# A fourth chunk pair with seven products, weight low parts made by accumulating transfers, and the first tile's parts ahead at stage borders

## Chip, core and metric

The kernel runs on one core of a Trainium2 chip. The metric is device time in microseconds (us) of one execution. The engines of the core are TensorE (PE in the profile), VectorE (DVE), ScalarE (ACT), GpSimd (POOL) and SyncE (SP); SyncE and GpSimd issue the DMA transfers here.

## The reference, cut to what matters

Two layers of an encoder over 256 tokens with 2048 features, all in float32:

```python
def hybrid_layer(x, ...):
    h = rmsnorm(x, pre_mix_norm)
    proj = h @ w_in                                     # 2048 -> 4176
    ...                                                 # attention, convolution, gated DeltaNet
    mix = jnp.concatenate([o_a, o_b, o_c], axis=-1) @ w_out
    x = x + rmsnorm(mix, post_mix_norm)
    h = rmsnorm(x, pre_ffn_norm)
    f = (jax.nn.silu(h @ w_gate) * (h @ w_up)) @ w_down # 2048 -> 5632 -> 2048
    return x + rmsnorm(f, post_ffn_norm)
```

`rmsnorm(x, w)` is `x * rsqrt(mean(x^2) + eps) * w`, with a mean per token and a gain `w` per feature.

## The kernel before, in words

**Products.** Every float32 operand is split into a high part (a rounded copy) and a low part (the rest): `hilo` (L327) lets ScalarE copy the high part (L328, CAST) and VectorE subtract it from the source (L329). A product of a 128x128 piece of activations with a 128x512 piece of weights is then three matmuls: high by high, low by high, high by low. The 256 tokens are two tiles of 128 (t = 0 and 1).

**Weights.** They stream from HBM once, as 512 KB transfers of two 128-row chunks into `ws` tiles (128x1024), issued by SyncE (L410). From a `ws` the two halves `wh` and `wl` are made. There are five slots each of `ws`, `wh` and `wl` (`WSB`, `WHB`, L42 and L43); whoever wants a new tile waits until a slot's last reader is done, and slots go round in the order in which they come free.

**Stages of a layer.** Input projection (`dense`, L337), the mixers, the output projection (`out_proj`, L1180, with `residual`, L477, at its end), the feed-forward's gate and up products, and `w_down` through `out_proj` again. At each border between stages the rows `xs` are transposed in groups of four chunks (`norm_quad`, L431): TensorE transposes (L435), and eight small instructions of 128x128 on ScalarE (L332) and VectorE (L333) apply the gain and split. The per-token factor of the norm is applied at the products' end. `norm_tok` makes all four groups of a tile at once.

**Gate and up.** The 5632 columns are 11 blocks of 512. The first block of a layer goes through `dense`; the other ten through `gate_up` (L1277; 20 calls in the two layers). Such a block takes the 16 chunks in eight pairs, in the order `QORDER` (L45). A pair multiplies two tiles of tokens by two chunks of the gate weight and two of the up weight: eight products, 24 matmuls. For the pairs in `FAST` (L44) it is done with seven products, 21 matmuls, as in Strassen's scheme: VectorE combines the weights (L1341 to L1347), and the sums of activations are made once per layer by `token_sums` (L1230), spread over other work. An eight-product pair takes two `wh`/`wl` slots, a seven-product pair four (in the order `r1`, `r2`, `r32`, `r14`). All 24 or 21 matmuls stand in one line, L1302. After the last pair the block's results are combined, SiLU and product applied, and the result is transposed later as a background task (`turn`, L1220), whose place the number `EARLY` (L46) decides for the first blocks.

**What sets the order.** The code is written as one instruction list; a scheduler orders each engine's instructions, and each engine then executes its own list in order, waiting on semaphores for the others.

Of the kernel before, what the change touches and what calls it, by code (L numbers as in the profile page):

```python
# [16 lines left out]
P = 128  # L17
# [3 lines left out]
NT = 2  # L21
# [22 lines left out]
FAST = (0, 1, 2)  # L44
QORDER = (4, 0, 5, 1, 6, 2, 7, 3)  # L45
EARLY = 2  # L46
# [7 lines left out]
def kernel(  # L54
# [282 lines left out]
    def dense(lhs, ks, n, load, evac, ch=2, need=None, pre=None, head=0, mid=None, tail=0,  # L337
              gain=None):
# [17 lines left out]
        def unit(u):  # L356
# [7 lines left out]
            with ExitStack() as order:  # L364
                if u < head:
                    for u0, ins in hold:
                        if u >= u0:
                            order.enter_context(tc.issue_after(ins.ins))
                if gain is None:
                    hilo(wh[:, 0:m * n], wl[:, 0:m * n], ws[:, 0:m * n])  # L370
                else:
                    for c in range(m):
                        sl = slice(c * n, (c + 1) * n)
                        hilo_col(wh[:, sl], wl[:, sl], ws[:, sl], vcol(*gain, kc[c]))
# [56 lines left out]
    def norm_quad(t, g, tiles, gain=None):  # L431
# [5 lines left out]
        if gain is None:  # L437
            hilo(hi, lo, ps)
        else:
# [53 lines left out]

    for l in range(DEPTH):
        hT = {}

        def more(g, t):

            for n in range(1, min(g + 2, 4)):
                if (n, 0) not in hT:  # L500
                    load_x(0, n)
                    norm_quad(0, n, hT, (0, PRE_MIX))
        hl = quad_lhs(hT, None if l else more)

        def mid_mix():
# [3 lines left out]
            norm_tok(1, hT, (l, PRE_MIX))  # L509
# [3 lines left out]
        if l:  # L513
            norm_tok(0, hT, (l, PRE_MIX))
        else:
# [664 lines left out]
        def out_proj(lhs, passes, w, wpm, rname, need=None):  # L1180
            parts = {}
            ssqp = [SM(4, "ssqp0"), SM(4, "ssqp1")]
            for i, ks in enumerate(passes):
                last = i == len(passes) - 1
                for nb in range(4):
# [3 lines left out]
                    def ev(t, ps):  # L1189
# [16 lines left out]
        out_proj(lmix, passes, w_out[l], wpm, "rm", need_mix)  # L1206


        h2 = {}
        h2l = quad_lhs(h2)  # L1210
        norm_tok(0, h2, (l, PRE_FFN))
# [18 lines left out]
        def token_sums():  # L1230
# [46 lines left out]
        def gate_up(fb, par):  # L1277
# [38 lines left out]

            def half(w, q):
# [14 lines left out]
            for n, q in enumerate(QORDER):  # L1332
# [58 lines left out]
        def first_block():  # L1391
# [6 lines left out]
            def ev_u(t, ps):  # L1398
# [4 lines left out]
                  mid=lambda: norm_tok(1, h2, (l, PRE_FFN)))  # L1403
# [13 lines left out]
        out_proj(quad_lhs(hid), [list(range(44))], w_down[l], wpf, "rd", lambda k: [f"hid{k // 4}"])  # L1417
    for t in range(NT):
# [34 lines left out]
```

## Time and profile before

| what | value |
|---|---|
| median of 3 runs | 2237.43 us (2236.23 to 2238.26) |
| the profiled execution's own time | 2236.18 us |
| its span, first to last instruction | 2234.4 us |
| outside the span | 1.8 us |
| mean granted TensorE clock | 0.998 of full speed |
| TensorE busy | 2201.4 us (99%), 10483 matmuls |
| VectorE / ScalarE / GpSimd busy | 79% / 54% / 2% |
| DMA | 407.76 MB, 182 GB/s over the span |

The first rows of a profile to read are the busy shares and the chain of work that ended last: they tell which engine sets the time. After that one stage at a time is read, with windows (busy time of each engine in a stretch), groups of instructions, and timelines.

### The profile page before, as it was taken

What the parts mean: (1) busy time and instruction counts of PE and PEld (TensorE: products, weight loads), DVE (VectorE), ACT (ScalarE), POOL (GpSimd) and SP (SyncE); (2) the same over time, 40 slices, a digit from 0 to 9 for tenths busy, and PEclk for the clock granted to TensorE, in tenths of its full rate; (3) what the DMA queues carried; (4) which work ended last, traced back from release to release, by engine and by line L of the source; (5) the groups of instructions that cost most, each with busy time, mean ns of one, the idle gap of its engine ahead of it and who ended that gap; (6) DMA issues with size and microseconds to landing.
All of it is one profiled execution on the core that took longest, in us unless ns stands there. A gap on an engine that the chain in (4) does not pass through costs nothing.

```text
span 2234.4 us, 29364 instructions
## 1 busy us (share of the span) xinstructions
PE 2201.4 (99%) x10483; PEld 1837.9 (82%) x10483; DVE 1765.2 (79%) x2943; ACT 1196.4 (54%) x1726; POOL 45.7 (2%) x93
## 2 busy tenths in 40 slices
PE   8999999999999999999999999999999999999998
PEld 7888887788888888888879888877788888888886
DVE  6777998899989897544486779978999998975444
ACT  6665545655555555444366655456555555554442
POOL 2000000000000000000000000000000000000000
PEclk9999999999999999999999999999999999999999
DMA  7554525546656656555556545245556566565553
GB/s 251 169 181 144 186 98 163 160 161 208 216 180 217 226 191 221 171 195 192 178 173 185 182 142 175 95 151 161 188 197 217 191 216 213 202 215 178 191 196 123
DMA packets 218546, 407.76 MB, mean 182 GB/s; under 512 B 17607, under 2 KB 30065, under 8 KB 218400
## 3 DMA queue, kind: packets, MB, share of 16 engines
q1 hardware_dynamic: 215360, 397.72, 54.3%
q0 software_dynamic: 3008, 8.16, 1.3%
q8 instruction: 82, 1.34, 0.2%
q14 instruction: 64, 0.52, 0.1%
q10 hardware_dynamic: 32, 0.01, 0.0%
HBM read 402.94 MB, written 2.90 MB: 182 GB/s over the span
## 4 chain that ended last, share of the span: by engine, by line
PE 91%; DVE 5%; DMA 1%; ACT 1%; issue 1%; SPq 0%; DVEq 0%; ACTq 0%; POOLq 0%
PE acc L1302 18%; PE tp L1302 18%; PE acc L352 16%; PE acc L354 16%; PE acc L353 16%; DVE wl L329 1%; DVE xs L482 1%; PE tp L1224 1%; DVE u L944 1%; DMA cd<-u 1%; PE tp L1045 0%; PE tp L796 0%; PE tp L789 0%; PE tp L1016 0%; ACT wh L328 0%
## 5 line engine op out<-in xcount | busy, mean ns | idle before, releaser
L328 ACT CAST wh<-ws 128x1024 fp32r<-128x1024 f32 (+3 forms) x820 | 813.8, 1010 | 803.5 <-PE acc L353 410.5
L329 DVE TENSOR_TENSOR wl<-ws,wh 128x1024 fp32r<-128x1024 f32 (+3 forms) x820 | 942.4, 1170 | 347.7 <-ACT wh L328 340.8
L352 PE MATMUL acc<-wh,u 128*128 128x512 f32 (+2 forms) x1792 | 696.8, 390 | 1.8 <-ACT u L332 1.8
L354 PE MATMUL acc<-wl,u 128*128 128x512 f32 (+2 forms) x1792 | 686.9, 383 | 2.5 <-DVE wl L329 2.5
L353 PE MATMUL acc<-wh,u 128*128 128x512 f32 (+2 forms) x1792 | 686.4, 383 | 3.0 <-DVE sm L264 2.7
L354 PEld LDWEIGHTS acc<-wl,u 128*128 128x128 f32 x1792 | 337.4, 188 | 67.2 <-DVE wl L329 4.7
L353 PEld LDWEIGHTS acc<-wh,u 128*128 128x128 f32 x1792 | 337.8, 189 | 65.8 <-DVE sm L264 3.6
L352 PEld LDWEIGHTS acc<-wh,u 128*128 128x128 f32 x1792 | 337.9, 189 | 63.3 <-ACT u L332 3.6
L1302 PE MATMUL tp<-wh,u 128*128 128x512 f32 x1220 | 375.9, 390 | 1.1 <-DVE u L329 0.9
L1302 PE MATMUL acc<-wh,u 128*128 128x512 f32 x1220 | 375.5, 389 | 0.0
L1302 PEld LDWEIGHTS tp<-wh,u 128*128 128x128 f32 x1220 | 228.4, 188 | 50.3 <-DVE u L329 1.7
L1302 PEld LDWEIGHTS acc<-wh,u 128*128 128x128 f32 x1220 | 228.7, 188 | 47.7 <-ACT wh L328 0.3
L1302 PE MATMUL acc<-wl,u 128*128 128x512 f32 x610 | 237.1, 389 | 0.0
L1302 PE MATMUL tp<-wl,u 128*128 128x512 f32 x610 | 236.4, 389 | 0.0
L1302 PEld LDWEIGHTS acc<-wl,u 128*128 128x128 f32 x610 | 114.5, 188 | 24.1 <-DVE wl L329 0.2
L1302 PEld LDWEIGHTS tp<-wl,u 128*128 128x128 f32 x610 | 114.4, 188 | 24.1
L944 DVE SCALAR_TENSOR_TENSOR u<-u,cols 128x241 f32<-128x241 f32 (+14 forms) x240 | 101.0, 469 | 0.0
L1340 ACT CAST wh<-ws 128x1024 fp32r<-128x1024 f32 x60 | 63.0, 1050 | 26.2 <-PE tp L1302 11.2
L332 ACT ACTIVATE u<-tp,cols 128x128 fp32r<-128x128 f32 (+2 forms) x116 | 40.1, 392 | 32.0 <-DVE u L333 28.3
L1341 DVE TENSOR_TENSOR wl<-ws,wh 128x512 fp32r<-128x512 f32 x60 | 41.1, 686 | 19.2 <-ACT wh L1340 18.9
L1325 ACT ACTIVATE u<-u,sm 128x512 f32<-128x512 f32 x40 | 28.8, 724 | 32.5 <-DVE u L1372 22.1
L333 DVE SCALAR_TENSOR_TENSOR u<-tp,cols,u 128x128 fp32r<-128x128 f32 (+2 forms) x116 | 39.6, 377 | 4.9 <-ACT u L332 4.9
(301 smaller groups left out, 1548.2 us busy)
## 6 DMA issues: line engine op xcount, KB each, us to landing
ws<-in_w_gate_dram SPq DMA_DIRECT2D x176, 512.0 KB, 4.9
ws<-in_w_up_dram SPq DMA_DIRECT2D x176, 512.0 KB, 4.8
ws<-in_w_down_dram SPq DMA_DIRECT2D x176, 512.0 KB, 3.6
ws<-in_w_in_dram SPq DMA_DIRECT2D x112, 512.0 KB, 4.4
ws<-in_w_out_dram SPq DMA_DIRECT2D x64, 512.0 KB, 3.7
ws<-in_w_ukv_dram SPq DMA_DIRECT2D x16, 512.0 KB, 3.7
ws<-in_w_uq_dram SPq DMA_DIRECT2D x16, 384.0 KB, 3.4
ws<-in_w_in_dram SPq DMA_DIRECT2D x10, 444.0 KB, 4.0
```

The source lines that it names most:

```text
L328: act.copy(out=hi, in_=src)
L329: dve.tensor_tensor(out=lo, in0=src, in1=hi.bitcast(F32), op=ALU.subtract)
L332: ins = act.activation(out=hi, in_=src, func=AF.Identity, scale=col)
L333: dve.scalar_tensor_tensor(out=lo, in0=src, scalar=col, in1=hi.bitcast(F32), op0=ALU.mult, op1=ALU.subtract)
L352: pe.matmul(o, xh, rh, start=(i == 0), stop=False)
L353: pe.matmul(o, xl, rh, start=False, stop=False)
L354: pe.matmul(o, xh, rl, start=False, stop=(i == len(ks) - 1))
L944: dve.scalar_tensor_tensor(out=o, in0=i, scalar=wc, in1=o, op0=ALU.mult, op1=ALU.add)
L1302: pe.matmul(o, a, b, start=count[i] == 1, stop=count[i] == total[i])
L1325: act.activation(out=sg[t], in_=x, func=AF.Silu, scale=rfb[0][:, t:t + 1])
L1340: act.copy(out=wh, in_=wg)
L1341: dve.tensor_tensor(out=wl[:, 0:512], in0=b11, in1=wh[:, 0:512].bitcast(F32), op=ALU.subtract)
```

## The change

- `FAST` gets pair 3 as a fourth seven-product pair. The order of pairs becomes 4, 0, 5, 1, 2, 6, 3, 7: pairs 1 and 2, both with seven products, now stand next to each other. `EARLY` becomes 1.
- In the four eight-product pairs the up weight's low part is not subtracted by VectorE any more. In `split_dma` ScalarE copies the high part as before (L1324), writes its negative into `wl` (L1325), and GpSimd issues a transfer of the same 512 KB of `w_up` from HBM that is added onto `wl` in place (L1326). That is 40 such transfers per layer. The up weight's `ws` is still loaded, for the high part.
- `norm_quad`: except for the first group of tile 0, VectorE multiplies the whole transposed 128x512 by the gain (L448) and `hilo` splits the result, one instruction each instead of four. The product is kept for `token_sums`, which then needs no addition of high and low part. Groups are made when a product asks for them (`ask`).
- At three borders the first group of the next stage's tile 0 (`after0`) stands ahead of tile 1's work in the last `dense`; at the kernel's end tile 0's stores do.

The diff, cut to its core:

```diff
-FAST = (0, 1, 2)
-QORDER = (4, 0, 5, 1, 6, 2, 7, 3)
-EARLY = 2
+FAST = (0, 1, 2, 3)
+QORDER = (4, 0, 5, 1, 2, 6, 3, 7)
+EARLY = 1
...
         if pre is not None:
             pre()
+        if after0 is not None:
+            after0()
         for t in range(1 if tail else 0, NT):
             evac(t, acc[t][:, 0:n])
...
-    def norm_quad(t, g, tiles, gain=None):
+    def gain_cols(l, i, c, n):
+        if l == 0 and i == PRE_MIX:
+            return col0[:, c:c + n]
+        o = voff[(l, i)] + c
+        return cols[:, 0, o:o + n]
+
+    def norm_quad(t, g, tiles, gain, keep=None):
 
         ps = TP()
         for c in range(4):
             pe.transpose(ps[:, c * P:(c + 1) * P], xs[:, t, (4 * g + c) * P:(4 * g + c + 1) * P], ident)
         hi, lo = U(F32R), U(F32R)
-        if gain is None:
-            hilo(hi, lo, ps)
-        else:
+        if g == 0 and t == 0:
             for c in range(4):
                 s = slice(c * P, (c + 1) * P)
-                ins = hilo_col(hi[:, s], lo[:, s], ps[:, s], vcol(*gain, 4 * g + c))
-                if not tiles:
-                    first_hi.append(ins)
+                ins = hilo_col(hi[:, s], lo[:, s], ps[:, s], vcol(*gain, c))
+                first_hi.append(ins)
+        else:
+            f = U()
+            dve.tensor_tensor(out=v3(f, 4), in0=v3(ps, 4), in1=bc(gain_cols(*gain, 4 * g, 4), 2, P), op=ALU.mult)
+            hilo(hi, lo, f)
+            if keep is not None:
+                keep[(g, t)] = f
         tiles[(g, t)] = (hi, lo)
 
-    def norm_tok(t, tiles, gain=None):
-        for g in range(4):
-            norm_quad(t, g, tiles, gain)
+    def ask(tiles, gain, load=None, keep=None):
+
+        def more(g, t):
+            for n in range(min(g + 2, 4)):
+                if (n, t) not in tiles:
+                    if load is not None and t == 0:
+                        load(0, n)
+                    norm_quad(t, n, tiles, gain, keep)
+        return more
...
+        hT, early = early, {}
+        more = ask(hT, (l, PRE_MIX), None if l else load_x)
+        hl = quad_lhs(hT, more)
...
-        def out_proj(lhs, passes, w, wpm, rname, need=None):
+        def out_proj(lhs, passes, w, wpm, rname, need, after0):
...
-                          tail=TAILG if last and nb == 3 else 0)
+                          **(dict(tail=TAILG, after0=after0) if last and nb == 3 else {}))
...
+        h2, F = {}, {}
+        out_proj(lmix, passes, w_out[l], wpm, "rm", need_mix, lambda: norm_quad(0, 0, h2, (l, PRE_FFN)))
+
+
+        more2 = ask(h2, (l, PRE_FFN), keep=F)
+        h2l = quad_lhs(h2, more2)
...
-                F = []
-                for t in range(NT):
-                    f = U()
-                    hi, lo = h2[(g, t)]
-                    dve.tensor_tensor(out=f, in0=hi.bitcast(F32), in1=lo.bitcast(F32), op=ALU.add)
-                    F.append(f.rearrange("p (q j n) -> p q j n", q=2, j=2))
-                    yield 0.6
+                if (g, 0) not in F:
+                    F[(g, 0)] = U()
+                    hi, lo = h2[(g, 0)]
+                    dve.tensor_tensor(out=F[(g, 0)], in0=hi.bitcast(F32), in1=lo.bitcast(F32), op=ALU.add)
+                f0, f1 = [F.pop((g, t)).rearrange("p (q j n) -> p q j n", q=2, j=2) for t in range(NT)]
...
+            def split_dma(src, w, q):
+
+                wh, wl = halves()
+                act.copy(out=wh, in_=src)
+                act.activation(out=wl, in_=wh.bitcast(F32), func=AF.Identity, scale=-1.0)
+                pool.dma_start(v3(wl, 2), w[2 * q * P:(2 * q + 2) * P, fb * 512:(fb + 1) * 512].rearrange(
+                    "(c p) n -> p c n", p=P), accum_op=ALU.add)
+                return [(wh[:, c:c + 512], wl[:, c:c + 512]) for c in (0, 512)]
...
-                    r2 = split(wu)
+                    r2 = split_dma(wu, w_up[l], q)
...
-        out_proj(quad_lhs(hid), [list(range(44))], w_down[l], wpf, "rd", lambda k: [f"hid{k // 4}"])
-    for t in range(NT):
-        for c in range(4):
-            sync.dma_start(out[t * P:(t + 1) * P, c * 512:(c + 1) * 512], xs[:, t, c * 512:(c + 1) * 512])
+
+        def store(t):
+            for c in range(4):
+                sync.dma_start(out[t * P:(t + 1) * P, c * 512:(c + 1) * 512], xs[:, t, c * 512:(c + 1) * 512])
+
+        out_proj(quad_lhs(hid), [list(range(44))], w_down[l], wpf, "rd", lambda k: [f"hid{k // 4}"],
+                 (lambda: norm_quad(0, 0, early, (l + 1, PRE_MIX))) if l + 1 < DEPTH else lambda: store(0))
+    store(1)
```

ScalarE's list in a block of the first layer, from the last weight copies of one seven-product pair to the next one. Before (`wh_6505` and `wh_6509` are the gate's and the up weight's high parts of pair 5, `wh_6541` the first of pair 1):

```order
L328 CAST wh_6473<-ws_6452 128x1024
L328 CAST wh_6505<-ws_6501 128x1024
L328 CAST wh_6509<-ws_6503 128x1024
L1340 CAST wh_6541<-ws_6537 128x1024
L328 CAST wh_6545<-ws_6539 128x512
```

After (`wh_5780`, `wh_5784` and `wl_5785` are pair 5's, `wh_5817` is pair 1's):

```order
L328 CAST wh_5748<-ws_5727 128x1024
L328 CAST wh_5780<-ws_5776 128x1024
L1324 CAST wh_5784<-ws_5778 128x1024
L1353 CAST wh_5817<-ws_5813 128x1024
L1325 ACTIVATE wl_5785<-wh_5784 128x1024
L328 CAST wh_5821<-ws_5815 128x512
```

The negative copy into `wl_5785` is new, and stands behind the first copy of the next pair.

TensorE's list at the first matmuls with pair 5's up weight (`wh_6509`/`wl_6510` before, `wh_5784`/`wl_5785` after; the u tiles are activations). Before:

```order
L1302 MATMUL acc_6438<-wh_6509,u_4284 128x512
L1302 MATMUL acc_6438<-wh_6509,u_4285 128x512
L1302 MATMUL acc_6438<-wl_6510,u_4284 128x512
L1302 MATMUL acc_6442<-wh_6509,u_4653 128x512
L1302 MATMUL acc_6442<-wh_6509,u_4654 128x512
L1302 MATMUL acc_6442<-wl_6510,u_4653 128x512
```

After:

```order
L1306 MATMUL acc_5713<-wh_5784,u_4237 128x512
L1306 MATMUL acc_5713<-wh_5784,u_4238 128x512
L1306 MATMUL acc_5717<-wh_5784,u_4569 128x512
L1306 MATMUL acc_5717<-wh_5784,u_4570 128x512
L1306 MATMUL acc_5713<-wl_5785,u_4237 128x512
L1306 MATMUL acc_5717<-wl_5785,u_4569 128x512
L1306 MATMUL acc_5713<-wh_5784,u_4237 128x512
```

The matmuls with the low part moved back by two places; the first of them, on `wl_5785`, now waits for a transfer of GpSimd's queue.

VectorE's list at the first border (end of the first layer's output projection), from the last residual of tile 0 (L482, after it L495). Before:

```order
L482 SCALAR_TENSOR_TENSOR xs_75<-u_3494,sm_4083,xs_75 128x512
L1195 TENSOR_TENSOR u_3495<-u_3495,acc_4026 128x512
L329 TENSOR_TENSOR wl_4228<-ws_4225,wh_4227 128x1024
L1199 TENSOR_TENSOR u_3495<-u_3495,u_2912 128x512
L262 TENSOR_SCALAR sm_4130<-sm_2918,sm_4127 128x1
L333 SCALAR_TENSOR_TENSOR u_4153<-tp_4147,cols_91,u_4152 128x128
L264 TENSOR_SCALAR sm_4131<-sm_4130 128x1
L267 TENSOR_SCALAR sm_4130<-sm_4130 128x1 x2
L269 SCALAR_TENSOR_TENSOR sm_4132<-sm_4131,sm_4130 128x1
L333 SCALAR_TENSOR_TENSOR u_4168<-tp_4162,cols_91,u_4167 128x128
L270 SCALAR_TENSOR_TENSOR sm_4131<-sm_4132,sm_4131 128x1
L333 SCALAR_TENSOR_TENSOR u_4153<-tp_4147,cols_91,u_4152 128x128
```

After:

```order
L495 SCALAR_TENSOR_TENSOR xs_75<-u_3466,sm_4055,xs_75 128x512
L1201 TENSOR_TENSOR u_3467<-u_3467,acc_3998 128x512
L333 SCALAR_TENSOR_TENSOR u_4101<-tp_4095,cols_91,u_4100 128x128
L448 TENSOR_TENSOR u_4153<-tp_4146,cols_91 128x512
L1205 TENSOR_TENSOR u_3467<-u_3467,u_2884 128x512
L333 SCALAR_TENSOR_TENSOR u_4101<-tp_4095,cols_91,u_4100 128x128
L262 TENSOR_SCALAR sm_4117<-sm_2890,sm_4114 128x1
L329 TENSOR_TENSOR u_4152<-u_4153,u_4151 128x512
L333 SCALAR_TENSOR_TENSOR u_4101<-tp_4095,cols_91,u_4100 128x128
L264 TENSOR_SCALAR sm_4118<-sm_4117 128x1
L267 TENSOR_SCALAR sm_4117<-sm_4117 128x1 x2
L269 SCALAR_TENSOR_TENSOR sm_4119<-sm_4118,sm_4117 128x1
```

The small splits of the next stage (L333) moved ahead, and one 128x512 multiplication with its subtraction (L448, L329) takes the place of the second group's four.

## Rows read from the trace of the kernel before

**Rows 1.** Page, part 1 (busy us, share, instructions) and part 2's row of the clock.

```profile
PE 2201.4 (99%) x10483; PEld 1837.9 (82%) x10483; DVE 1765.2 (79%) x2943; ACT 1196.4 (54%) x1726; POOL 45.7 (2%) x93
...
PEclk9999999999999999999999999999999999999999
```

**Rows 2.** Page, part 4: shares of the chain that ended last.

```profile
PE 91%; DVE 5%; DMA 1%; ACT 1%; issue 1%; SPq 0%; DVEq 0%; ACTq 0%; POOLq 0%
```

**Rows 3.** Windows: a gate/up block, three borders, the end; columns in the first line.

```profile
core 0: us, PE busy (x) PEld busy (x) DVE busy (x) ACT busy (x) POOL busy (x), PEclk, DMA share, GB/s
1799.20:1840.68 41.48, 41.48 (x185) 34.35 (x184) 37.72 (x47) 22.86 (x25) 0.00 (x0) 1.00 0.59 202
390.00:416.00 26.00, 22.45 (x109) 17.02 (x107) 22.79 (x65) 14.24 (x36) 0.00 (x0) 1.00 0.32 94
1108.00:1132.00 24.00, 21.78 (x105) 16.80 (x104) 19.52 (x54) 11.59 (x28) 0.20 (x1) 1.00 0.36 109
1500.00:1524.00 24.00, 21.64 (x100) 16.58 (x99) 21.29 (x60) 14.30 (x35) 0.00 (x0) 0.93 0.27 83
2222.00:2234.40 12.40, 3.28 (x15) 2.39 (x13) 8.42 (x24) 0.69 (x2) 0.00 (x0) 0.74 0.45 169
```

**Rows 4.** Chain in order of time, inside a block: start, us, what.

```profile
1799.20 12.24 PE acc L1302 x54
```

**Rows 5.** Groups in the block 1799.20 to 1840.68: busy us, mean ns, idle before.

```profile
L329 DVE TENSOR_TENSOR wl<-ws,wh 128x1024 fp32r<-128x1024 f32 x17 | 20.1, 1222 | 1.9 <-ACT wh L328 1.6
...
L328 ACT CAST wh<-ws 128x1024 fp32r<-128x1024 f32 x16 | 16.3, 1050 | 13.3 <-DVE ws L1345 10.7 <-DMA ws<-in_w_gate_dram 1.2 <-DMA ws<-in_w_up_dram 0.5
...
L1341 DVE TENSOR_TENSOR wl<-ws,wh 128x512 fp32r<-128x512 f32 x3 | 2.1, 687 | 1.4 <-ACT wh L1340 1.4
```

**Rows 6.** TensorE's timeline at the second product of a fast pair.

```profile
1817.17 0.39 PE L1302 MATMUL acc<-wl,u 128*128 128x512 f32 x1
1817.40 0.62 PE L1302 MATMUL tp<-wh,u 128*128 128x512 f32 x2
1817.86 0.39 PE L1302 MATMUL tp<-wl,u 128*128 128x512 f32 x1
```

**Rows 7.** ScalarE's timeline there, with the idle time before and its releaser.

```profile
1815.15 4.00 ACT L328 CAST wh<-ws 128x1024 fp32r<-128x1024 f32 x4 [4.40 <-DVE ws L1345]
1819.06 1.05 ACT L1340 CAST wh<-ws 128x1024 fp32r<-128x1024 f32 x1
```

**Rows 8.** Page, part 6: loads, KB each, median us from issue to landing.

```profile
ws<-in_w_up_dram SPq DMA_DIRECT2D x176, 512.0 KB, 4.8
ws<-in_w_down_dram SPq DMA_DIRECT2D x176, 512.0 KB, 3.6
```

**Rows 9.** SyncE's loads (L410) in the stretch 1758 to 1965.

```profile
DMA to landing us min/median/max: 3.5/4.9/6.0
```

**Rows 10.** GpSimd's loads of 256 KB (L490), 1800 to 1900.

```profile
L490 POOL DMA_DIRECT2D u<-in_post_ffn_norm_dram x4: 537/538/539, 1855.1 to 1897.2; - x4
...
DMA to landing us min/median/max: 3.3/3.5/3.7
```

**Rows 11.** Page, part 3: SyncE's queue, packets, MB, share of 16 engines.

```profile
q1 hardware_dynamic: 215360, 397.72, 54.3%
```

**Rows 12.** TensorE's timeline at the first border.

```profile
399.02 2.14 PE L435 MATMUL tp<-ident,xs 128*128 128x128 f32 x16
402.04 0.50 PE L352 MATMUL acc<-wh,u 128*128 128x512 f32 x1 [0.89 <-ACT u L332]
403.15 0.50 PE L353 MATMUL acc<-wh,u 128*128 128x512 f32 x1 [0.61 <-DVE sm L264]
...
408.54 0.66 PE L435 MATMUL tp<-ident,xs 128*128 128x128 f32 x4 [1.28 <-DVE u L333]
409.93 0.50 PE L354 MATMUL acc<-wl,u 128*128 128x512 f32 x1 [0.73 <-DVE wl L329]
```

**Rows 13.** VectorE's timeline there.

```profile
405.49 2.73 DVE L482 SCALAR_TENSOR_TENSOR xs<-u,sm,xs 128x512 f32<-128x512 f32 x4
```

More of the change, by code (lines that the diff above doesn't have):

```diff
@@ L337, in dense @@
     def dense(lhs, ks, n, load, evac, ch=2, need=None, pre=None, head=0, mid=None, tail=0,
-              gain=None):
+              after0=None):
         acc = [psa.tile([P, 512], F32, tag="acc", name="acc") for _ in range(NT)]
@@ L368, in unit @@
                             order.enter_context(tc.issue_after(ins.ins))
-                if gain is None:
-                    hilo(wh[:, 0:m * n], wl[:, 0:m * n], ws[:, 0:m * n])
-                else:
-                    for c in range(m):
-                        sl = slice(c * n, (c + 1) * n)
-                        hilo_col(wh[:, sl], wl[:, sl], ws[:, sl], vcol(*gain, kc[c]))
+                hilo(wh[:, 0:m * n], wl[:, 0:m * n], ws[:, 0:m * n])
             if need is not None:
@@ L491, in post_weight @@
         return w
+    early = {}
     for l in range(DEPTH):
[L495 to L503, printed above, removed]
+        hT, early = early, {}
+        more = ask(hT, (l, PRE_MIX), None if l else load_x)
+        hl = quad_lhs(hT, more)
         def mid_mix():
@@ L508, in mid_mix @@
                     load_x(1, c)
-            norm_tok(1, hT, (l, PRE_MIX))
+            more(0, 1)
             if l == 0:
                 bg.add("setup", setup())
-        if l:
-            norm_tok(0, hT, (l, PRE_MIX))
-        else:
+        if l == 0:
             norm_quad(0, 0, hT, (0, PRE_MIX))
@@ L1202, in out_proj @@
                     dense(lhs, ks, 512, wload(w, nb * 512, 512), ev, need=need,
-                          tail=TAILG if last and nb == 3 else 0)
+                          **(dict(tail=TAILG, after0=after0) if last and nb == 3 else {}))
         passes = [list(range(8)), [12, 13, 14, 15, 8, 9, 10, 11]]
[L1206 to L1211, printed above, removed]
+        h2, F = {}, {}
+        out_proj(lmix, passes, w_out[l], wpm, "rm", need_mix, lambda: norm_quad(0, 0, h2, (l, PRE_FFN)))
+        more2 = ask(h2, (l, PRE_FFN), keep=F)
+        h2l = quad_lhs(h2, more2)
         rfb = []
@@ L1236, in token_sums @@
                 fast = [q for q in range(2) if 2 * g + q in FAST]
-                F = []
-                for t in range(NT):
-                    f = U()
-                    hi, lo = h2[(g, t)]
-                    dve.tensor_tensor(out=f, in0=hi.bitcast(F32), in1=lo.bitcast(F32), op=ALU.add)
-                    F.append(f.rearrange("p (q j n) -> p q j n", q=2, j=2))
-                    yield 0.6
+                if (g, 0) not in F:
[3 more added lines that the diff above has]
+                f0, f1 = [F.pop((g, t)).rearrange("p (q j n) -> p q j n", q=2, j=2) for t in range(NT)]
                 d = U()
-                dve.tensor_tensor(out=d.rearrange("p (q j n) -> p q j n", q=2, j=2), in0=F[0], in1=F[1],
+                dve.tensor_tensor(out=d.rearrange("p (q j n) -> p q j n", q=2, j=2), in0=f0, in1=f1,
                                   op=ALU.subtract)
@@ L1260, in token_sums @@
                 w = v3(s4[:, 0:256], 2)
-                dve.tensor_tensor(out=v[:, 0:m, 0], in0=F[1][:, qs, 0], in1=F[1][:, qs, 1], op=ALU.add)
-                dve.tensor_tensor(out=v[:, 0:m, 1], in0=v[:, 0:m, 0], in1=F[0][:, qs, 0], op=ALU.subtract)
-                dve.tensor_tensor(out=w[:, 0:m], in0=F[0][:, qs, 1], in1=v[:, 0:m, 1], op=ALU.subtract)
+                dve.tensor_tensor(out=v[:, 0:m, 0], in0=f1[:, qs, 0], in1=f1[:, qs, 1], op=ALU.add)
+                dve.tensor_tensor(out=v[:, 0:m, 1], in0=v[:, 0:m, 0], in1=f0[:, qs, 0], op=ALU.subtract)
+                dve.tensor_tensor(out=w[:, 0:m], in0=f0[:, qs, 1], in1=v[:, 0:m, 1], op=ALU.subtract)
                 yield 1.2
@@ L1402, in first_block @@
                   pre=lambda: rfb.append(row_rstd(l, "rf")), head=HEADG,
-                  mid=lambda: norm_tok(1, h2, (l, PRE_FFN)))
+                  mid=lambda: more2(0, 1))
             bg.add("sums", token_sums())
```

2 lines of the change are left out of this document (removed).

## The prediction

> **What bounds the kernel now.** First the busy shares: TensorE works 2201.4 us of a span of 2234.4, at the full clock in every slice [rows 1], and 91% of the chain that ended last is TensorE [rows 2]. Then one gate/up block, in windows: TensorE is busy for the whole 41.48 us, VectorE for 37.72, ScalarE for 22.86, the DMA engines for 0.59 of it [rows 3]. Inside it the chain is TensorE alone, 54 matmuls in 12.24 us [rows 4], 0.2267 us each; the 183 matmuls of a block (five pairs of 24, three of 21) are 41.48 us. So in the feed-forward a block costs its matmuls, and everything else is hidden as long as it is in time. Last the borders, where TensorE does idle: 3.55, 2.22 and 2.36 us in the three windows [rows 3].
>
> The profiled execution took 2236.18 us (its span plus 1.8), 1.25 below the median of 2237.43. I sum against it.
>
> **Fourth seven-product pair.** Three matmuls fewer in each of the 20 blocks: 60 x 0.2267 = -13.6 us, since TensorE sets a block's length. A block's matmuls then take 180 x 0.2267 = 40.81 us. VectorE's share changes little: the new pair costs it seven 128x512 instructions of 0.69 us and two of 1.22 [rows 5], 7.3 in all, and six 1.22 us subtractions go (of ten in eight-product pairs four are left), also 7.3: still about 37.7 us, now of 40.8. `token_sums` has sums for one more pair and seven additions fewer per layer, beside other work: nothing.
>
> **Borders.** At the first one TensorE waits 0.89 and 0.61 us for the first splits, then 1.28 and 0.73 for splits [rows 12] that stand on VectorE behind a residual of 2.73 us [rows 13]; the order now puts the first two groups ahead of it. The three windows' idle time is 8.1 us; the gain lies between 0 and 8, as each split still follows its transposition. I take half, -4. The early stores at the end: nothing, since that stretch is VectorE's (8.42 of 12.4 us [rows 3]).
>
> **The added transfer.** This term decides. In an eight-product pair VectorE made the up weight's low part with one subtraction, hidden. Now it needs the high copy, a negative copy, and a GpSimd transfer of 512 KB. The transfer can't start early: `wl` must be a free slot. So each one has a budget, from GpSimd's issue to the moment when TensorE wants `wl`. I work it out from the order of the matmuls.
>
> How slots come free is seen in the trace. The fourth of four casts begins at 1818.10 (1815.15 + 4.00 - 1.05) [rows 7], 0.08 us after the two matmuls that end at 1818.02 [rows 6]. These are the last readers of a seven-product pair's `r2`, which is freed earliest of its four. Casts in a row start every 0.98 us (3 steps in 2.95), and the last ends 1.05 after its start. A matmul ends 0.16 us after the next one has begun (0.39 - 0.23).
>
> Name the pairs of a block 4s, 0F, 5s, 1F, 2F, 6s, 3F, 7s (s for eight products, F for seven).
> - 5s: its up weight takes 0F's `r2` slot, free after the fifth of 21 matmuls. From there 16 of 0F, 12 of the gate half and 4 on the high part stand ahead of the first matmul on `wl`: 32 x 0.2267 - 0.16 = 7.1 us. ScalarE needs 0.08 + 2 x 0.98 + 1.05 = 3.1 for copy, 1F's first copy (which the order puts between) and negative copy; with 0.1 for the hand-overs 3.9 us are left.
> - 7s takes 3F's `r2` in the same way, with 30 matmuls ahead: 6.6 - 3.2 = 3.45.
> - 6s follows two adjacent F pairs. 2F's first copy gets its slot only when 5s's last high matmul is done; from there to the first matmul on 6s's `wl` there are 64 (1 + 21 + 21 + 12 + 4 + 5 of 3F put ahead): 14.35 us. The chain is the copy (1.13), six VectorE instructions at 0.6 to 0.7 (3.8, as one pair's steps depend on each other), then two `r` copies, gate, up and 3F's copy, and the negative copy: 10.9 us in all. 3.3 are left.
> - 4s: ScalarE is still at 7s's chain, but 52 matmuls stand ahead: 5.5.
>
> If the transfer takes T from issue to landing, a block loses the sum of max(0, T - budget).
>
> What is T? No row shows an adding transfer, so bounds. From below: SyncE's fastest 512 KB in this stage, 3.5 us [rows 9], which loses 0.25 us a block, 5 in all. GpSimd's own transfers of 256 KB take 3.3 to 3.7, median 3.5, in the same stage [rows 10]; another 256 KB at the queue's rate (397.72 MB in 54.3% of the span, 328 GB/s [rows 11]) adds 0.8: 4.3, 45 us. The addition has to read the old `wl` too, 512 KB more, 1.6 us: 5.9, 149 us. And in this stage SyncE's loads take 4.8 where those of `w_down` take 3.6 [rows 8]; 1.2 for such queueing on top gives 7.1, 245 us. Below nothing it can't come: VectorE's subtraction was hidden, so its absence gives TensorE nothing. I take 5.1, midway between 4.3 and 5.9, as these start from GpSimd's own row: 5s 1.2, 7s 1.65, 6s 1.8, 4s 0, together 4.65 us a block, x 20 = +93.
>
> For the second read the Trainium skill has a rule ("Collectives: The Full Stack", The bandwidth ceiling): an adding transfer reads two sources, and moves at half the rate of a copy. By it alone the term would be the 149, by a plain copy the 45; no run here shows which yet.
>
> GpSimd has nothing else in these blocks (0.00 busy [rows 3]) but the four loads of the norm's gain at the end, now queued behind the last adding transfer and wanted only at the end of `w_down`: nothing. The extra 2 MB a block are 6.4 us at 328 GB/s in 41 us where the engines are 0.59 busy: room on the average.
>
> **Small.** VectorE has two adjacent F pairs now. By the chain above the low part of 2F's `r32` is ready about 7.2 us after 5s's end and wanted at 7.1: 0 to 0.3 us a block, I take 0.15, +3 us. `EARLY` moves work of the same length: nothing.
>
> **Sum.** 2236.2 - 13.6 - 4 + 93 + 3 = 2314.6 us: **2315**, 3.5% slower.
>
> **The rivals.**
>
> *The transfer is hidden (the other side).* If T is at most 3.6, a block loses 0.45 us or less, and the sum is 2236.2 - 17.6 + 0 to 12, so 2218.6 to 2231; without any stall, 2219. The point from which it decides: 17.6 - 3 = 14.6 us of gain are used up at 0.73 us of stall a block, 2T - 6.75 = 0.73, T = 3.74. For it: SyncE's fastest load of this size in the stage took 3.5 [rows 9]. Against it: half the bytes on GpSimd's queue took as much as that [rows 10], with nothing to add. The Trainium skill speaks for it ("DMA: Bandwidth & Descriptors", Anatomy of one DMA, SWDGE path): a GpSimd transfer takes about 2.0 us plus its bytes at 436 GB/s, an estimate of 3.2 us for 512 KB, under every budget, and the time would be 2219. For 256 KB that rule gives 2.6 where the trace has 3.3 to 3.7, so the trace doesn't agree.
>
> *VectorE becomes the bound.* It would be busy 37.7 of 40.8 us; if the adjacent F pairs make it late by one instruction of 1.22 us [rows 5] a block, with the transfer hidden, that is 24 us: 2243. For it: the chain over two F pairs has no slack at `r32`. Against it: three pairs' slack lies behind.
>
> *The transfer is very long or the clock falls.* T over 6.25 means over 2400. Also, with stalls in every block TensorE's granted clock may fall: at the border of 1500 it idled 2.36 of 24 us with the clock at 0.93, though at the two others, as idle, it stayed at 1.00 [rows 3].
>
> That the change doesn't do what it says I give no chance: the order shows the transfers and the 60 matmuls gone.
>
> **How the numbers follow.** A measurement of this kernel can tell about 0.2% (4.5 us) from no change. The forecast's case, T from 4.0 to 6.25 (27 to 177 us, so 2249 to 2399), gets 0.60; the hidden transfer 0.20; VectorE, with T just over 3.6 beside it (2233 to 2249), 0.07; the very long transfer 0.13. Faster 0.20; within 0.2% (2233 to 2242) most of the third case, 0.05; slower the rest, 0.75. The range takes in the first three cases and leaves out the last, with the rim of the others: 2218 to 2400. The likeliest case's own range is 2249 to 2400.
>
> **What would show it.** In the changed kernel's trace: 183 against 180 matmuls a block, and a block's length of 40.8 us plus the stalls. Right: TensorE idle at matmuls on `wl`, released by a DMA of `w_up`, up to three times a block, largest at 6s, none at 4s; GpSimd's transfers at 4 to 6 us; VectorE still near 37.7 us a block. Wrong: blocks of 40.8 without such idle time, transfers under 3.7 us; or the idle time ended by VectorE; or slots handed out in another order, which would change all four budgets. At the borders the idle time should fall from 8.1 to about 4 us.

## The result: 2538.59 us, 13.5% slower

| | us |
|---|---|
| before, median of 4 runs | 2237.39 |
| changed kernel, median of 4 runs (2536.78 to 2543.09) | 2538.59 |
| ratio, 95% interval | 1.1349 (1.1336 to 1.1363) |
| forecast (range) | 2315 (2218 to 2400) |

The sign was right; the time lies outside the range, and the loss is 301 us where 78 were forecast. One of the five executions of run e12 below took 5698.48 us, for a reason that stays open, and its ratio leaves it out as slow. The profile after begins with the page: busy us by engine, the granted clock by slices, GpSimd's queue (packets, MB, share of 16 engines), and the adding transfer (KB each, median us to landing).

```profile
PE 2304.3 (91%) x10423; PEld 1887.1 (74%) x10423; DVE 1771.2 (70%) x2933; ACT 1288.3 (51%) x1762; POOL 141.5 (6%) x173
...
PEclk9999999989888989999999999998888988889999
...
q0 software_dynamic: 24768, 50.11, 10.9%
...
wl<-in_w_up_dram POOLq DMA_DIRECT2D x80, 512.0 KB, 7.8
```

Against [rows 1] there are 60 matmuls fewer, as the change says, but TensorE is busy for 103 us more and idle for 231 us in place of 33. The clock is below full in many slices, all in the gate/up stages. The adding transfer takes 7.8 us in the median from issue to landing. What TensorE waited for (us in total, times, longest):

```profile
PE acc L1306 <- DMA wl<-in_w_up_dram: 98.0, 35, 5.3
...
PE tp L1306 <- DMA wl<-in_w_up_dram: 96.5, 31, 5.1
```

194.5 us in 66 waits in 20 blocks. The only other waits at L1306 are 4.8 us for ScalarE's activations (L1338); none there ended with VectorE. One block shows them. GpSimd's issues (start, us, idle before and what ended it), for 6s, 7s, 4s and 5s in this order:

```profile
1969.64 1.19 POOL L1326 DMA_DIRECT2D wl<-in_w_up_dram  x1 [22.16 <-ACT wl L1325]
1985.10 1.22 POOL L1326 DMA_DIRECT2D wl<-in_w_up_dram  x1 [14.27 <-ACT wl L1325]
1988.79 1.20 POOL L1326 DMA_DIRECT2D wl<-in_w_up_dram  x1 [2.48 <-ACT wl L1325]
2004.03 1.20 POOL L1326 DMA_DIRECT2D wl<-in_w_up_dram  x1 [14.04 <-ACT wh L328]
```

and TensorE's matmuls on those `wl`:

```profile
1978.05 1.19 PE L1306 MATMUL tp<-wl,u 128*128 128x512 f32 x2 [4.79 <-DMA wl<-in_w_up_dram]
...
1991.19 0.47 PE L1306 MATMUL tp<-wl,u 128*128 128x512 f32 x1 [0.96 <-DMA wl<-in_w_up_dram]
...
1996.81 0.47 PE L1306 MATMUL acc<-wl,u 128*128 128x512 f32 x1 [0.37 <-DMA wl<-in_w_up_dram]
...
2010.71 0.70 PE L1306 MATMUL acc<-wl,u 128*128 128x512 f32 x2 [2.97 <-DMA wl<-in_w_up_dram]
```

6s: issued at 1969.64, TensorE ready at 1978.05 - 4.79 = 1973.26, so 3.6 us were to spare and the transfer took 8.3. 5s: ready at 2007.74, 3.7 to spare. These are the budgets of the prediction, 3.3 and 3.9. 7s and 4s had 5.1 and 7.6 to spare, where the prediction had 3.45 and 5.5. A part of the reason is in the clock. Windows of the same block (length, busy us and count of PE, PEld, DVE, ACT, POOL, then the granted clock, DMA share and GB/s):

```profile
1974.00:1978.00 4.00, 0.00 (x0) 0.00 (x0) 1.96 (x2) 1.94 (x3) 0.00 (x0) 0.91 1.07 259
1978.00:1980.00 2.00, 1.95 (x5) 1.59 (x6) 0.00 (x0) 0.00 (x0) 0.00 (x0) 0.50 0.87 323
1980.00:1982.00 2.00, 2.00 (x6) 1.55 (x5) 0.10 (x1) 0.54 (x1) 0.00 (x0) 0.50 0.08 26
1982.00:1984.00 2.00, 2.00 (x6) 1.58 (x5) 1.12 (x1) 1.76 (x3) 0.00 (x0) 0.50 0.26 30
1984.00:1986.00 2.00, 2.00 (x10) 1.58 (x10) 0.74 (x2) 1.71 (x2) 0.90 (x1) 0.98 0.93 314
1986.00:1990.00 4.00, 4.00 (x19) 3.18 (x17) 3.68 (x6) 3.33 (x5) 1.51 (x2) 1.00 0.96 201
1990.00:1994.00 4.00, 3.04 (x14) 2.36 (x13) 3.31 (x6) 0.72 (x1) 0.00 (x0) 1.00 1.04 314
```

After the 4.79 us of idle time TensorE's matmuls run at half clock, the lower of the two levels, until about 1984, 6 in 2 us where there are 10 at full clock. After the 0.96 us wait at 1991 the clock is still 1.00. So a long wait is paid twice. The slow matmuls end just before 7s's issue at 1985.10: seven of them, each 0.2 us late, stand between the start of its high copy (1981.46) and that issue, so TensorE comes to 7s's low part up to 1.4 us later. In 4s's stretch, from 1988.79 on, the clock is full, and 7s's own wait of 0.96 us is a part of what 4s has more.

### The profile page after: what moved, and what is told of

It reads as the page before. It is cut to its first block, busy times and chain, and to the rows that moved or that the text cites. A ratio compares the mean times of both kernels' runs of the same rounds, so it can differ in the third digit from the quotient of the medians.

```text
span 2535.4 us, 29736 instructions
## 1 busy us (share of the span) xinstructions
PE 2304.3 (91%) x10423; PEld 1887.1 (74%) x10423; DVE 1771.2 (70%) x2933; ACT 1288.3 (51%) x1762; POOL 141.5 (6%) x173
## 3 DMA queue, kind: packets, MB, share of 16 engines
q8 instruction: 82, 1.34, 0.2%
## 5 line engine op out<-in xcount | busy, mean ns | idle before, releaser
L329 DVE TENSOR_TENSOR wl<-ws,wh 128x1024 fp32r<-128x1024 f32 (+3 forms) x760 | 863.8, 1153 | 447.5 <-ACT wh L328 329.4
L328 ACT CAST wh<-ws 128x1024 fp32r<-128x1024 f32 (+3 forms) x760 | 743.3, 994 | 801.9 <-PE acc L354 409.0
L1306 PE MATMUL acc<-wh,u 128*128 128x512 f32 x1200 | 394.4, 416 | 0.0
L1306 PE MATMUL tp<-wh,u 128*128 128x512 f32 x1200 | 392.7, 414 | 0.0
L1306 PE MATMUL acc<-wl,u 128*128 128x512 f32 x600 | 253.7, 435 | 100.8 <-DMA wl<-in_w_up_dram 98.0
L1306 PE MATMUL tp<-wl,u 128*128 128x512 f32 x600 | 254.3, 436 | 98.9 <-DMA wl<-in_w_up_dram 96.5
L1306 PEld LDWEIGHTS acc<-wh,u 128*128 128x128 f32 x1200 | 245.6, 205 | 54.9
L1306 PEld LDWEIGHTS tp<-wh,u 128*128 128x128 f32 x1200 | 244.8, 204 | 54.9
L1306 PEld LDWEIGHTS acc<-wl,u 128*128 128x128 f32 x600 | 124.6, 211 | 143.4 <-issue 104.9
L1306 PEld LDWEIGHTS tp<-wl,u 128*128 128x128 f32 x600 | 124.5, 211 | 141.1 <-issue 96.3
L1326 POOL DMA_DIRECT2D wl<-in_w_up_dram x80 | 95.7, 1197 | 1412.5 <-ACT wl L1325 1101.3
L1324 ACT CAST wh<-ws 128x1024 fp32r<-128x1024 f32 x80 | 83.8, 1048 | 117.2 <-issue 109.0
L1353 ACT CAST wh<-ws 128x1024 fp32r<-128x1024 f32 x80 | 83.8, 1048 | 114.8 <-issue 111.4
L1325 ACT ACTIVATE wl<-wh 128x1024 fp32r<-128x1024 f32 x80 | 84.4, 1055 | 0.1
```

What stands on the lines that cost most here:

```text
L328: act.copy(out=hi, in_=src)
L329: dve.tensor_tensor(out=lo, in0=src, in1=hi.bitcast(F32), op=ALU.subtract)
L1306: pe.matmul(o, a, b, start=count[i] == 1, stop=count[i] == total[i])
L1324: act.copy(out=wh, in_=src)
L1325: act.activation(out=wl, in_=wh.bitcast(F32), func=AF.Identity, scale=-1.0)
L1326: pool.dma_start(v3(wl, 2), w[2 * q * P:(2 * q + 2) * P, fb * 512:(fb + 1) * 512].rearrange("(c p) n -> p c n", p=P), accum_op=ALU.add)
```

## The experiments

Medians, with ratios to the kernel before measured beside them. "Changed" is the changed kernel with one edit.

| run | edit | us | ratio (95%) |
|---|---|---|---|
| e9 | changed, no transfer at all | 2253.33 | 1.0073 (1.0057 to 1.0090) |
| e12 | e9, old order of pairs | 2255.91 | 1.0085 (1.0069 to 1.0101) |
| e2 | changed, plain transfer | 2434.67 | 1.0884 (1.0864 to 1.0904) |
| e10 | changed, half the bytes | 2515.51 | 1.1240 (1.1217 to 1.1262) |
| e3 | changed, seven slots | 2444.72 | 1.0929 (1.0905 to 1.0953) |
| e7 | changed, negative copy earlier | 2564.36 | 1.1469 (1.1448 to 1.1490) |
| e11 | changed, old order of pairs | 2557.30 | 1.1426 (1.1403 to 1.1450) |
| e4 | changed, transfer in pair 4 only | 2344.32 | 1.0480 (1.0461 to 1.0499) |
| e1 | changed, VectorE subtracts | 2284.86 | 1.0209 (1.0195 to 1.0223) |
| e6 | e1, old order of pairs | 2287.19 | 1.0230 (1.0214 to 1.0245) |
| e8 | changed, GpSimd subtracts | 2336.93 | 1.0453 (1.0439 to 1.0467) |
| e5 | borders alone | 2233.81 | 0.9989 (0.9980 to 0.9998) |

### What the transfers cost: e9 and e12

e9 takes the transfer out and leaves everything else:

```diff
-                pool.dma_start(v3(wl, 2), w[2 * q * P:(2 * q + 2) * P, fb * 512:(fb + 1) * 512].rearrange(
-                    "(c p) n -> p c n", p=P), accum_op=ALU.add)
```

> The changed kernel without the adding transfers; the negative copy stays as the low part, so the low product of those weights is wrong and VectorE's load is the changed kernel's. This is the changed kernel less the one suspected cost. Theory (the transfers cost all of it; VectorE with 37.7 of 40.8 us isn't the bound): blocks of 40.8 to 41.2 us, 2216 to 2228. Rival (part of the loss is VectorE and the adjacent seven-product pairs even at this load): blocks over 41.8 us with TensorE's idle time released by ScalarE or VectorE, 2237 or more.

2253.33: the transfers cost 285 us (2538.59 - 2253.33). Between the two spans, 2535.4 and 2250.1, TensorE is busy for 101 us less (2304.3 against 2203.3) and idle for 184 less. So 101 us of the 285 are the low clock, the rest idle time. The trace agrees: the changed kernel's TensorE is busy for 203 us at the granted clock 0.50, e9's for 3. But 16 us above before is left, where 60 matmuls and the borders should have put it 16 below. The rival holds: part of the loss is not the transfer. Two blocks of e9, in windows:

```profile
1928.39:1970.94 42.55, 41.67 (x180) 33.55 (x180) 37.92 (x50) 27.30 (x32) 0.00 (x0) 1.00 0.59 198
1886.00:1928.39 42.39, 41.39 (x180) 33.61 (x181) 37.74 (x50) 27.59 (x33) 1.07 (x2) 1.00 0.63 211
```

42.4 to 42.6 us where 180 matmuls are 40.8. I put that down to the two adjacent seven-product pairs, and set them apart (e12):

```diff
-QORDER = (4, 0, 5, 1, 2, 6, 3, 7)
+QORDER = (4, 0, 5, 1, 6, 2, 7, 3)
```

> As the run without adding transfers (the low part of those up weights stays the negative copy), with the pairs in the old order, where no two seven-product pairs stand side by side. Theory (without transfers, what is left of the loss is VectorE in the two adjacent seven-product pairs: some 12.2 us of its work in a row): the loss against 180 matmuls a block goes, blocks of 40.8 to 41.1 us, 2216 to 2226, faster than before. Rival (VectorE with 37.7 of 40.8 us a block is late in any order): 2240 to 2260.

2255.91: that theory fell, the order changes nothing. A block of e12:

```profile
1746.32:1788.91 42.59, 41.36 (x180) 33.63 (x180) 37.41 (x50) 27.63 (x32) 0.00 (x0) 1.00 0.59 198
```

Once a block TensorE waits 1.23 us, in another place (some 0.3 us more of that wait lies under the modelled end of the matmul before it). Followed back there: TensorE's row, then ScalarE's and VectorE's.

```profile
1788.91 1.20 PE L1306 MATMUL tp<-wh,u 128*128 128x512 f32 x4 [1.23 <-ACT wh L328]
```

```profile
1787.82 2.95 ACT L328 CAST wh<-ws 128x1024 fp32r<-128x1024 f32 x3 [4.84 <-DVE ws L1356]
```

```profile
1778.52 0.69 DVE L1352 TENSOR_TENSOR wl<-ws,wh 128x512 fp32r<-128x512 f32 x1 [1.16 <-ACT wh L1351]
...
1783.92 1.40 DVE L1338 SCALAR_TENSOR_TENSOR u<-u,sm 128x512 f32<-128x512 f32 x2
1785.24 0.68 DVE L329 TENSOR_TENSOR wl<-ws,wh 128x512 fp32r<-128x512 f32 x1
...
1787.05 0.68 DVE L1356 TENSOR_TENSOR ws<-ws 128x512 f32<-128x512 f32 x1
```

The matmul waits for the copy of 1787.82, the copy for VectorE's combination of the weights. VectorE began that pair at 1778.52 (it waited 1.16 us for ScalarE's first copy, held by its slot), and between its steps does the previous block's sums and products, which end at 1785.3. So VectorE, 37.4 of 42.6 us busy on the average, is late by one to two us just where its work is densest. In e9 that is at the second of the adjacent pairs, in e12 at the first pair after the block's end. No run takes VectorE's work away alone, so this is read from the chain. ScalarE's added negative copies are the rival; against them speaks e1 below, which has none of them and more VectorE work, and is 32 us slower still. Why the kernel before doesn't meet it, with three such pairs, I infer only from the count: a fourth pair brings denser VectorE work and more turns of the five slots.

### What the transfer takes: e2 and e10

e2: a plain transfer at the same place; the low part is then the whole weight.

```diff
-                    "(c p) n -> p c n", p=P), accum_op=ALU.add)
+                    "(c p) n -> p c n", p=P).bitcast(F32R))
```

> The changed kernel with a plain transfer in place of the adding one: same bytes, same queue, same place; the low part is then the whole weight, so the output is not the reference's. Theory (the addition reads the old contents too, 512 KB more at 328 GB/s, 1.6 us): transfers of about 6.2 us in place of 7.8, idle time at wl of some 5 us a block in place of 9.8, time 2340 to 2440. Rival (GpSimd's queue itself is slow, the addition is free): transfers still 7.5 to 8 us, time 2520 to 2545. Other rival (all that is above SyncE's 4.6 is the addition): transfers of 4.6 us, time 2240 to 2290.

The median is 6.2 us, as the first theory said, and the time is at the upper end of its range (idle time at `wl` 6.3 us a block, not 5). So the second read is worth 104 of the 285 us; a plain transfer in this place still costs 181 over e9. GpSimd's queue and the transfer on e2's page:

```profile
q0 software_dynamic: 24768, 50.11, 6.9%
...
wl<-in_w_up_dram POOLq DMA_DIRECT2D x80, 512.0 KB, 6.2
```

The queue's share times the span is 168 us in e2 and 276 in the changed kernel; 29 of each are other transfers (1.3% of the span of before). For 80 transfers that is 1.7 us of the 16 engines each for a plain one, and 3.1 for an adding one. The Trainium skill has a rule for the adding step of a collective ("Collectives: The Full Stack", The bandwidth ceiling): the add needs two source reads, and so comes to half the rate of a copy. This trace agrees for a transfer that adds into `wl`: 1.8 times here.

The time to landing depends on what was issued ahead. When 7s's transfer is issued at 1985.10, two loads of SyncE, issued 2.0 and 2.6 us earlier, are under way. One transfer of the changed kernel there, then one of e2 (1958.7, the same place):

```profile
DMA to landing us min/median/max: 6.0/6.0/6.0
```

```profile
DMA to landing us min/median/max: 4.2/4.2/4.2
```

6.0 adding and 4.2 plain. When 6s's is issued at 1969.64, three loads are under way, issued 1.6 to 2.7 us earlier, and it takes 8.3. What the queues moved then (packets, MB, share of 16 engines; q1 is SyncE's, q0 GpSimd's), first in 1970 to 1973, then in 1974 to 1977.5:

```profile
q1 hardware_dynamic: 441, 0.85, 95.6%
```

```profile
q0 software_dynamic: 264, 0.51, 81.0%
q1 hardware_dynamic: 174, 0.33, 26.5%
```

For 3 us GpSimd's queue moves nothing, though its transfer is issued; then it moves its 512 KB. So the transfer stands behind the loads issued ahead of it. All 80 of the changed kernel bear this out: with two transfers under way at the issue the median is 6.0 us (22 of them), with three 7.9 (46), with four 8.3 (12). So the prediction's two bounds from GpSimd's own row, 4.3 plain and 5.9 adding, are what the places with the fewest loads ahead show; at the others about 2 us come on top, not 1.2.

e10 adds only the first 256 KB of each part:

```diff
-                pool.dma_start(v3(wl, 2), w[2 * q * P:(2 * q + 2) * P, fb * 512:(fb + 1) * 512].rearrange(
-                    "(c p) n -> p c n", p=P), accum_op=ALU.add)
+                pool.dma_start(wl[:, 0:512], w[2 * q * P:(2 * q + 1) * P, fb * 512:(fb + 1) * 512], accum_op=ALU.add)
```

> The changed kernel with adding transfers of the first 256 KB only (the second half of those low parts stays the negative copy, so the output is not the reference's). Theory (a transfer costs what it exceeds its budget by; the bytes cost 3.1 us of the 7.8): 5.5 to 6 us each, idle time at wl of 3.5 to 5.5 us a block in place of 9.8, the clock seldom low as no stall reaches 4 us, 2290 to 2345. Rival (a fixed price of each such transfer, whatever its size): over 2480.

Transfers are shorter, median 6.2, and 4.2 at 7s (issued at 1966.99):

```profile
DMA to landing us min/median/max: 4.2/4.2/4.2
```

but 2515.51 is a miss for the theory: only 23 us gained. It lies in the rival's range, but the rival's fixed price isn't what the trace shows, since 7s fell from 6.0 to 4.2. Idle time at `wl` stayed near 9 us a block. At 5s and 6s, the crowded places, the transfers took 6.1 to 7.8 us, most of it behind the loads ahead, and the order that the scheduler made put the waiting matmul 2 (5s) and 4 (6s) places earlier, by count 0.45 and 0.9 us less to spare. So waits near 4 us remained there, and the low clock with them (0.956 on the mean, 0.951 in the changed kernel). Bytes alone don't settle it.

### Starting earlier: e3, e7, e11, e4

e3 gives seven slots:

```diff
-WHB = 5
+WHB = 7
-UB = 64
+UB = 56
```

> The changed kernel with seven wh and wl slots in place of five (and 56 small tiles in place of 64, for the room). Theory (each transfer starts only when its slot comes free, so two more slots let it start 3 to 5 us earlier): transfers still near 7.8 us, idle time at wl falls from 9.8 to under 3 us a block, time 2220 to 2290. Rival (the transfers are bound by the DMA engines or by GpSimd's queue): they get longer by what they start earlier, time over 2450.

2444.72: better by 94 us, outside both ranges and far from hidden (idle time at `wl` 6.7 us a block). The transfers now take 8.0 in the median; 4s's is issued 2.8 to 3.8 us behind 7s's and takes 8.0 to 9.5. Each of the theories is half right: earlier starts help, and neighbours lengthen each other.

e7 takes the negative copy from the loaded weight, so that ScalarE makes it ahead of the next pair's copy:

```diff
-                act.activation(out=wl, in_=wh.bitcast(F32), func=AF.Identity, scale=-1.0)
+                act.activation(out=wl, in_=src, func=AF.Identity, scale=-1.0)
```

> The changed kernel with the negative copy taken from the loaded weight and not from the high copy, so that on ScalarE it stands right behind the high copy, ahead of the next pair's first copy. Same transfers. Theory (what counts is the time from issue against the budget, and ScalarE's list sets the issue): each issue about 1 us earlier, and by TensorE's order up to 6 matmuls more ahead of the first low one: 1 to 1.7 us less idle time at three transfers a block, and less time at the low clock after them, time 2400 to 2465. Rival (bound by the transfers' own throughput): transfers longer by as much, time still 2520 to 2545.

2564.36, slower, and above the rival's range too. Issues of 7s and 4s are now mostly 2 us apart, the median transfer takes 8.9 and 4s's mostly 10 to 11. What the earlier issue gave, the queue took back, and a little more: the rival's mechanism holds.

e11 is the changed kernel in the old order of pairs, with no two adding transfers in a row.

> The changed kernel with the pairs in the old order (4, 0, 5, 1, 6, 2, 7, 3): no two adding transfers follow each other (7 and 4 did, 2 to 4 us apart) and no two seven-product pairs. Theory (time from issue against budget, where neighbours in the queue lengthen it): transfers of 6.5 to 7.5 us and of even length, budgets near 3.9 in all four places, idle time 10 to 14 us a block, 2500 to 2600, so not better. Rival (the new order makes the loss, by its adjacent pairs or by the collision): under 2400.

2557.30, with 11.0 us idle a block, both as expected. The transfers are shorter and less even than expected, 5.7 to 8.6 with a median of 6.1, but now all four places wait, 1.2 to 4.6 us.

e4 keeps the transfer in pair 4 only, where I had counted the longest budget.

```diff
-                    r2 = split_dma(wu, w_up[l], q)
+                    r2 = split_dma(wu, w_up[l], q) if q == 4 else split(wu)
```

> The changed kernel with the adding transfer in pair 4 alone, VectorE's subtraction in pairs 5, 6 and 7: 20 transfers in place of 80. Pair 4 has the longest budget by my count, 5.5 us. Theory (a transfer costs what it is longer than its budget): 6 to 8 us each, idle time of 0.5 to 2.5 us a block, 10 to 50 us in all, no fall of the clock for such short stalls, time 2229 to 2270. Rival (any transfer of this kind holds TensorE up for a fixed time, or takes SyncE's loads out of time): a quarter of the 320 us, 2290 to 2310.

2344.32, outside both. TensorE waits 3.4 to 5.8 us there in 16 of the 20 blocks, and the clock did fall (0.977 on the mean). ScalarE's timeline shows why the waits are long:

```profile
1842.06 1.06 ACT L1324 CAST wh<-ws 128x1024 fp32r<-128x1024 f32 x1 [0.97 <-DMA ws<-in_w_up_dram]
1844.05 1.06 ACT L1353 CAST wh<-ws 128x1024 fp32r<-128x1024 f32 x1 [0.94 <-DMA ws<-in_w_gate_dram]
1845.01 1.33 ACT L1338 ACTIVATE u<-u,sm 128x512 f32<-128x512 f32 x2
1846.25 1.04 ACT L1325 ACTIVATE wl<-wh 128x1024 fp32r<-128x1024 f32 x1
```

The copy into `wh` is done at 1843.1, the negative copy (L1325) at 1847.3: the list has the next pair's copy between, which waits 0.94 us for its load, and two activations. 2.5 us were left, not 5.5. Budgets are a matter of the order the scheduler makes for that very kernel.

### VectorE and GpSimd in its place: e1, e6, e8

e1 is the changed kernel with VectorE's subtraction again:

```diff
-                    r2 = split_dma(wu, w_up[l], q)
+                    r2 = split(wu)
```

> The changed kernel with the up weight's low part subtracted by VectorE again, no adding transfer; everything else of the change stays. Theory (the adding transfer alone cost the time, as it takes 7.8 us where 3.3 to 5.5 are to spare): all 312 us of longer blocks go, blocks of 40.8 us, time 2216 to 2225. Rival (the two adjacent seven-product pairs, or the borders, hold TensorE up): 2260 or more, with TensorE's idle time released by VectorE.

2284.86, in the rival's range: the transfer isn't what makes this variant slow, since it has none. A block of it:

```profile
1875.22:1919.27 44.05, 41.60 (x181) 33.19 (x181) 41.87 (x54) 23.59 (x28) 1.06 (x2) 1.00 0.62 203
```

VectorE has four subtractions more than in the changed kernel, 41.87 us in a block, which becomes 44.05 long. So the transfers did take work from the engine that becomes the bound with a fourth seven-product pair. e6, the same with the old order, tells whether the adjacent pairs matter:

> As the run with VectorE's subtraction (four seven-product pairs, no transfer), but with the pairs in the old order, where no two seven-product pairs stand side by side. Theory (VectorE's whole work is too long: 37.7 us of before, plus four subtractions more than the changed kernel has, some 42.3 of 40.8 us): the loss stays, blocks of 42.5 to 44 us, time 2255 to 2290. Rival (the adjacent pairs are what holds TensorE up): blocks of 40.8 to 41.2, time 2215 to 2225.

2287.19, as the theory said: they don't.

e8 lets GpSimd subtract:

```diff
-                act.activation(out=wl, in_=wh.bitcast(F32), func=AF.Identity, scale=-1.0)
-                pool.dma_start(v3(wl, 2), w[2 * q * P:(2 * q + 2) * P, fb * 512:(fb + 1) * 512].rearrange(
-                    "(c p) n -> p c n", p=P), accum_op=ALU.add)
+                pool.tensor_tensor(out=wl, in0=src, in1=wh.bitcast(F32), op=ALU.subtract)
```

> The changed kernel with the up weight's low part subtracted by GpSimd itself, in place of negative copy and adding transfer. GpSimd's subtraction of 128x256 takes 0.735 us in the trace of before, so some 2.9 us for 128x1024 (estimate, by elements), under every budget of the transfer (3.3 to 5.5), and ScalarE has one copy less. Theory (only the time from issue to low part matters): blocks of 40.8 us, no idle time at wl, time 2216 to 2228, faster than before. Rival (GpSimd and VectorE slow each other down when both read): VectorE's instructions get longer, it becomes the bound as without the transfer, 2250 to 2330.

GpSimd takes about 2.73 us, near the estimate, but 2336.93 is above even the rival's range, and its mechanism holds. VectorE's groups of e8 (1900 to 1990) and GpSimd's group:

```profile
L329 DVE TENSOR_TENSOR wl<-ws,wh 128x1024 fp32r<-128x1024 f32 x23 | 29.8, 1339 | 4.1 <-ACT wh L328 4.1
L1352 DVE TENSOR_TENSOR wl<-ws,wh 128x512 fp32r<-128x512 f32 x8 | 14.0, 1750 | 1.8 <-ACT wh L1351 1.8
```

```profile
L1325 POOL TENSOR_TENSOR wl<-ws,wh 128x1024 fp32r<-128x1024 f32 x80 | 218.3, 2728 | 1091.2 <-ACT wh L1324 1075.7 <-PE tp L1306 15.5
```

L1352, the step of VectorE that runs beside GpSimd's, takes 1.75 us on the mean where the same step took 0.69 [rows 5], and the mean of the 1024-wide ones goes from 1.22 to 1.34.

### The borders alone: e5

Before's pairs, order, `EARLY` and subtraction, with the change's borders and splits.

> Only the borders of the change: groups split with one gain multiplication, made on demand, the first group of tile 0 and the last stores ahead, no additions in the sums; three seven-product pairs, their old order, EARLY of 2 and VectorE's subtraction as before. Prediction's term: a gain of 4 us, 2228 to 2237, TensorE idle some 4 us at the three borders in place of 8.1. Rival (each group still waits for its own transposition and split): within 2 us of before, idle time 7 to 8 us.

2233.81, 2.75 us better than before, with an interval that excludes no change by little. The three borders:

```profile
390.00:416.00 26.00, 23.54 (x108) 16.82 (x107) 21.80 (x54) 9.18 (x17) 0.00 (x0) 1.00 0.34 106
1104.00:1128.00 24.00, 22.31 (x102) 17.03 (x101) 18.15 (x43) 9.16 (x15) 0.20 (x1) 1.00 0.48 142
1496.00:1520.00 24.00, 21.76 (x100) 15.69 (x99) 20.99 (x52) 8.61 (x17) 0.00 (x0) 1.00 0.38 121
```

They leave 2.46, 1.69 and 2.24 us idle, 6.4 in all against 8.1 [rows 3]: the time is in the theory's range, the idle time between the theory's 4 and the rival's 7 to 8. This is the only version here that is faster than before, by 0.1%.

## Why the prediction was wrong, step by step

Put together: -13.6 for the matmuls, -2.75 for the borders (e5), +32 for VectorE (e9 less these two from 2237.7), +285 for the transfers (changed kernel less e9): 301. The +32 is what e9 shows without transfers. In the changed kernel itself no wait at L1306 ends with VectorE, so the waits for the transfers cover its lateness, and the two terms are not side by side in one trace.

The signs that the prediction named came: idle time at `wl`, released by a DMA of `w_up`, some three times a block, largest at 6s and little at 4s. The mechanism was right for the waits; its sizes, and the clock, were not.

- *Fourth pair, 60 matmuls:* right.
- *VectorE's load:* 37.7 us a block, right, but that it is therefore hidden was wrong. It has slack on the average and is late at one place a block. The term of +3 was mis-sized by a factor of ten (+32, in e9); the rival with VectorE had 24 and the mechanism, put on the adjacent pairs, which e12 and e6 don't bear out. So even with no transfer at all the change is 0.7% slower than before.
- *Borders:* -4 forecast, -2.75 measured, inside the bounds.
- *Length of the transfer:* the step that failed most. The bounds from GpSimd's own row were right for the places with the fewest loads ahead (4.2 and 6.0 against 4.3 and 5.9), but I took a value between them, half a second read, when the second read is there in full; and the queueing behind SyncE's loads, which I kept for the far end of the range at 1.2, is about 2 at 6s and 4s. Median 7.8, taken 5.1, highest bound 7.1. "Room on the average" was the argument for it: in a block of 40.8 us the sixteen loads (1.6 us each) and four adding transfers (3.1) would fill 38 us of the engines' time. With 7.8 and the prediction's budgets its own rule gives 15 us a block, 301 in all; that this is near the measured 285 is chance, as only 9.7 us a block were idle at `wl`, and the clock made up for the rest.
- *Budgets:* 5s and 6s as worked out (3.7 and 3.6 against 3.9 and 3.3). 7s and 4s came out longer, behind slow matmuls (7s) and behind 7s's wait (4s); that these stretch the budgets is argued, not tried apart.
- *Clock:* left out of the sum and named only in the last rival, with 0.13 beside a very long transfer. It is 101 us. That rival is what came, in both its halves: the median of 7.8 lies above its 6.25, and the clock fell.

## What to carry to other kernels

Price a transfer that adds with both reads and with what else is in the queues at that very place, and then ask whether TensorE's waits also cost it its clock (101 us here). An engine at 92% of the bound isn't hidden by that alone: look where its work is dense, not at the average. Before moving work off a busy engine, try the change with that work simply left out (e9 here); if the time is no better then, moving the work will hardly make it so.

## What the runs showed that I had not expected

- The clock's share: after the wait of 4.79 us the granted clock was 0.50 from 1978 to 1984, after that of 0.96 us it was 1.00; over the run 101 us.
- GpSimd needs 1.20 us to issue an adding transfer of 512 KB, 0.70 for a plain one (1197 and 703 ns), and of two adding transfers 2 us apart the second mostly takes 10 to 11 us (e7).
- A transfer on GpSimd's queue stands behind the loads that SyncE issued before it: for 3 us of 6s's 8.3 its queue moved nothing.
- A GpSimd subtraction more than doubles a VectorE step that runs beside it (0.69 to 1.75 us).
